# A conformer layer's gated tiles turned by VectorE through DRAM instead of by TensorE, with three smaller moves

## The chip, the core and the metric

One core of one Trainium2 chip runs the whole program. The metric is device time in microseconds (us), from runs of the whole program; the profile is one execution in which every instruction of every engine was recorded. The engines named below are PE (TensorE), DVE (VectorE), ACT (ScalarE), POOL (GpSimd) and SP (SyncE, which here only issues DMAs). Each engine works through its own instructions in order. DMAs issued by SP run in the hardware queue q1, those issued by ACT in q10.

## The reference, cut to what matters

Two layers on 256 latent and 256 context tokens (together the 512 rows below) with 1024 channels. Layer 0 mixes tokens with a conformer convolution, layer 1 with a bidirectional chunkwise mLSTM; each is followed by a squared-ReLU MLP.

```python
def conformer_conv(u, rows, w_pw1, b_pw1, w_dw, b_dw, ln_g, ln_b, w_pw2, b_pw2):
    a = u @ w_pw1 + b_pw1
    a = a[..., :CONV_DIM] * jax.nn.sigmoid(a[..., CONV_DIM:])
    a = dwconv(a, w_dw)                   # the latent part in rows of 64
    a = jax.nn.silu(layer_norm(a + b_dw, ln_g, ln_b))
    return a @ w_pw2 + b_pw2

def mlstm_chunk_scan(q, k, v, i_pre, f_pre, state):
    lf = jax.nn.log_sigmoid(f_pre)
    ...
        bcum = jnp.cumsum(lfc, axis=-1)
        dlog = bcum[..., :, None] - bcum[..., None, :] + ic[..., None, :]
    ...
```

## The kernel before, in words

**Products.** All weights are float32. A big weight arrives as `raw`, a piece of 1 MB (128 partitions x 2048). ACT casts each half of it to `wh` (L151), DVE forms the rest `wl` from `raw` and `wh` (L152), and PE does three matmuls for each product (L182, L185, L186, and L213 to L215 in the output-gate product of layer 1). `raw` has a few buffers, so SP can issue the load of a piece only when an older one was read for the last time.

**What sets the order.** The kernel is written as a program in one order; a tile scheduler then sets every engine's own order, and puts in the waits. `tc.issue_after(x)` holds an instruction behind x. Within an engine nothing overtakes: if SP's next DMA waits for PE, the DMAs behind it wait too.

**Start.** `vecs` holds all bias and norm vectors, 408 values on each partition. Its first 64 (L117) are the first DMA of the program, and the other 344 (172 KB; L657) are issued after the second start step. Behind that come eight start steps (`start0` to `start2`): for each 128 channels SP loads a piece of `ada_w`, of `xT` and of `pw1a`; PE makes the modulation (L344, tile `fl`), DVE and ACT build `u`, and PE adds to the first four groups of the pointwise product `pw1`.

**Pointwise product and gate.** The product gives 16 tiles of 128 channels x 512 tokens: for each f in 0 to 7 a gate (even group) and a value (odd group). `pw1_epi` passes the gate through a sigmoid (L791, ACT) and then multiplies the value with it (L795, DVE): that makes the gated tile `a`, channels on the partitions. The convolution works on the other layout, tokens on the partitions: tile `A` (128 x 4 x 1024). `turn(f, a)` does it: four PE transposes of 128x128 into PSUM (L806, tile `ln`), one ACT copy into `A` (L807). For f = 0 to 2 the call is put into the list `turns` and taken out when the next group ends. f = 0 to 3 are the first half of the channels (h = 0), f = 4 to 7 the second (h = 1).

**Convolution.** After f = 3 (and after f = 7) the half goes through forward transforms along the tokens: matmuls of `A` with tables (L830, `ge`, `lt`, `tab`, then L835), a product with the transformed taps on DVE (L849), and back (L860). `taps` builds the transformed filter by matmuls with a table (L741) and two ACT operations (L742). The modulation parts that come later in layer 0 (`ada_g1`, `ada_s2`) are matmuls L344 on `raw` pieces of `ada_w`, put between these steps; four more pieces of `ada_w` go into parts of `A` that are free again (L943).

**Layer 1.** The values of attention are already turned by DVE in 32x32 blocks into the tile `res` (L1261), stored in DRAM (`v_dr`, four DMAs by ACT for each set, L1265) and loaded again by SP. In the attention stage a generator `decay` makes log-decays from the gates on ACT and DVE (L1413 to L1428), their cumulative sums on PE (L1435, L1436), copies these back (L1437), scans (L1448), stores a row in DRAM (`ng_dr`) and loads it spread over the partitions (L1510, tile `L`). Each `yield` in `decay` gives the turn to the output-gate product (weights `wo`), which runs beside it, a half group of it per step. The residual `R`, 1 MB in the tile `res`, is loaded from `r_dr` at the start of the second of four parts, (h, d) = (0, 1) (L1573).

Of the kernel before, what the change touches and what calls it, by code (L numbers as in the profile page):

```python
# [8 lines left out]
F32 = mybir.dt.float32  # L9
# [62 lines left out]
def hybrid_kernel(ctx: ExitStack, tc: tile.TileContext, xT, vecs_d, wdw_d, ada0_w, ada_w, wg_d, pw1a, pw1, pw2, w1_0, w2_0,  # L72
# [12 lines left out]
    def nm(s):  # L85
        uid[0] += 1
        return f"{s}_{uid[0]}"
# [13 lines left out]
    def psum(tag="mm"):  # L101
        return pp.tile([P, 512], F32, tag=tag, name=nm(tag), bufs={"mm": 3, "ln": 2, "fl": 1, "cv": 2}[tag])
# [10 lines left out]


    vecs = con.tile([P, NV], F32, name="vecs")
    NV0 = _OFF["ada_b1"][0]
    nc.sync.dma_start(vecs[:, :NV0], vecs_d[:, :NV0])  # L117

    def V(name, i=0, n=1):
        o = _OFF[name][0]  # L120
# [533 lines left out]
    start1(0)  # L654
    idle(spare, 5)
    start0(1)
    nc.sync.dma_start(vecs[:, NV0:], vecs_d[:, NV0:])  # L657
    for f in range(DT):
        start2(f, (0,))
        if f + 1 < DT:  # L660
# [118 lines left out]
                              qtr.rearrange("p (b j c) -> p j b c", b=4, j=4)[:, :, :, 0:16])  # L779


    A = padp.tile([P, 4, D], F32, name="A")
    Y = [[U() for _ in range(2)] for _ in range(4)]
    bst = con.tile([P, 4, 2, 6], F32, name="bst")
    hold, mark = {}, {}

    def pw1_epi(m, ps):
        f, gate = m // 2, m % 2 == 0
        if gate:
            sg = tmp("E")  # L790
            mark["gate"] = nc.scalar.activation(sg, ps, AF.Sigmoid, bias=V("b_pw1", DT + f)).ins  # L791
            hold[f] = sg
            return
        a = hold.pop(f)
        nc.vector.scalar_tensor_tensor(a, ps, V("b_pw1", f), a, op0=ALU.add, op1=ALU.mult)  # L795
        if f < 3:
            turns.append(lambda: turn(f, a))
        else:
            turn(f, a)

    turns = []

    def turn(f, a):
        tr = psum("ln")
        for b in range(4):
            mark["tr"] = nc.tensor.transpose(tr[:, b * P:(b + 1) * P], a[:, b * P:(b + 1) * P], ident).ins  # L806
        nc.scalar.copy(A[:, :, f * P:(f + 1) * P], tr.rearrange("p (b c) -> p b c", b=4))  # L807
        if f == 3:
            with tc.issue_after(mark["tr"]):
                ada_g1.mm(first, range(4, 8))  # L810
            for tt in range(2):
                whole(tt, [psum() for _ in range(2)])
# [96 lines left out]
    ada_g1, ada_s2 = Ada(0, 4, 2), Ada(0, 6, 6)  # L909

    def pw1_next(m, ps):
        while turns:
            turns.pop(0)()
        if m == 3:
            first.extend(ada_load(0, 4))
            ada_g1.mm(first, range(4))
        if m == 11:
            ada_s2.mm(half + ada_load(0, 6 + ada_s2.n, halves=(1,)))
            with tc.issue_after(mark["gate"]):
                nc.scalar.activation(warm, eps, AF.Sqrt)  # L920
        if m in (5, 6):
            with tc.issue_after(lastmm[0]):
                back(0, m - 3, psum("cv"))
        pw1_epi(m + KO0, ps)
        if m in (1, 2):
            taps(m - 1)
        if m in (4, 6):
            unit = ada_g1 if m == 4 else ada_s2
            blocks = ada_load(0, unit.u0 + unit.n)
            with tc.issue_after(lastmm[0]):  # L930
                unit.mm(blocks)
        if m in (4, 5):
            whole(m - 2, [psum(), psum("ln")], True)
        if m == 5:
            ada_g1.end()
        if m == 8:
            for i, tag in enumerate("SLSL"):
                half.append(tmp(tag))
                nc.sync.dma_start(half[i], ada_w[0, 6 + ada_s2.n, 0, :, i * 512:(i + 1) * 512])
        if m == 10:  # L940
            pw2_raw.extend(raw_load(pw2[g, 0]) for g in range(2))
            for i in range(4):
                nc.sync.dma_start(A[:, i, 0:512], ada_w[0, 10, 0, :, i * 512:(i + 1) * 512])  # L943
# [244 lines left out]
    for _ in side:  # L1188
        pass

    def rows_tile():
        return xp.tile([P, 2, D], F32, tag="res", name=nm("res"), bufs=1)

    r_dr = dp.tile([P, 2, D], F32, name="r_dr")
    R = rows_tile()
    for f in range(0, DT, 2):
# [195 lines left out]
    def decay(_):  # L1392
        gT = tmp("L")
        nc.scalar.copy(gT, gps)
        yield
        gk = psum("ln")
        for b in range(4):
            nc.tensor.matmul(gk[:, b * 16:(b + 1) * 16], gT[:, b * P:(b + 1) * P], foldg, start=True, stop=True)
        gs = tmp("S")[:, 0:64].rearrange("p (b c) -> p b c", b=4)
        nc.vector.tensor_tensor(gs, gk[:, 0:64].rearrange("p (b c) -> p b c", b=4),  # L1400
                                VA("b_gate").rearrange("p (b c) -> p b c", b=4), op=ALU.add)
        gb_ = [tmp("L"), tmp("E"), tmp("E")]
        g8 = [gb_[i // 3][:, (i % 3) * 4 * NG:(i % 3 + 1) * 4 * NG].rearrange("p (b c) -> p b c", b=4) for i in range(8)]
        ig, fg, bsb, ex, up1, cor, lf, fa = g8
        nc.vector.memset(ig, 0.0)
        nc.vector.memset(fg, 0.0)
        for d in range(2):
            nc.vector.tensor_copy(ig[:, :, 32 * d:32 * d + 4], gs[:, :, 8 * d:8 * d + 4])
            nc.vector.tensor_copy(fg[:, :, 32 * d:32 * d + 4], gs[:, :, 8 * d + 4:8 * d + 8])


        nc.vector.scalar_tensor_tensor(fa, fg, -1.0, fg, op0=ALU.mult, op1=ALU.max)
        nc.scalar.activation(ex, fa, AF.Exp, scale=-1.0)  # L1413
        nc.vector.tensor_scalar(up1, ex, 1.0, None, op0=ALU.add)
        nc.vector.scalar_tensor_tensor(cor, up1, -1.0, ex, op0=ALU.add, op1=ALU.subtract)
        nc.scalar.activation(lf, up1, AF.Ln)
        nc.vector.reciprocal(up1, up1)
        nc.vector.tensor_tensor(cor, cor, up1, op=ALU.mult)
        nc.vector.tensor_tensor(lf, cor, lf, op=ALU.subtract)
        nc.vector.tensor_scalar(fa, fg, 0.0, None, op0=ALU.min)  # L1420
        nc.vector.tensor_tensor(lf, lf, fa, op=ALU.add)

        nc.vector.memset(up1, 0.0)
        for d, (b0, b1, b2, b3) in ((0, (0, 1, 2, 3)), (1, (1, 0, 3, 2))):
            c = slice(32 * d, 32 if d == 0 else NG)
            nc.vector.tensor_copy(up1[:, b1, c], lf[:, b0, c])
            nc.vector.tensor_tensor(up1[:, b2, c], up1[:, b1, c], lf[:, b1, c], op=ALU.add)
            nc.vector.tensor_tensor(up1[:, b3, c], up1[:, b2, c], lf[:, b2, c], op=ALU.add)  # L1428
        yield
        yield  # L1430
        bps = psum("ln")
        for d, cum in ((0, upper), (1, lower)):
            c = slice(32 * d, 32 if d == 0 else NG)
            reg = bps[:, 0:4 * NG].rearrange("p (b c) -> p b c", b=4)[:, :, c]
            nc.tensor.matmul(reg, cum, lf[:, :, c], start=True, stop=False)  # L1435
            nc.tensor.matmul(reg, ones, up1[:, :, c], start=False, stop=True)  # L1436
        nc.vector.tensor_copy(bsb, bps[:, 0:4 * NG].rearrange("p (b c) -> p b c", b=4))  # L1437
        nc.vector.tensor_tensor(acol, ig, bsb, op=ALU.subtract)

        yield  # L1440
        aT = psum("ln")
        for b in range(4):
            nc.tensor.transpose(aT[:NG, b * P:(b + 1) * P], acol[:, b, :], ident)
        aR, mR = tmp("S"), tmp("S")
        nc.vector.tensor_copy(aR[:32, :], aT[:32, :])
        nc.vector.tensor_copy(aR[32:NG, LO], aT[32:NG, LO])
        nc.vector.tensor_copy(aR[32:NG, HI], aT[32:NG, T - 1:C - 1:-1])
        nc.vector.tensor_tensor_scan(mR[:NG, :], aR[:NG, :], aR[:NG, :], 0.0, op0=ALU.max, op1=ALU.max)  # L1448
        nc.vector.tensor_scalar(negm[:32, :], mR[:32, HI], -1.0, None, op0=ALU.mult)
        nc.vector.tensor_scalar(negm[32:NG, :], mR[32:NG, T - 1:C - 1:-1], -1.0, None, op0=ALU.mult)  # L1450
        nc.scalar.dma_start(ng_dr, negm)
        bsbs.append(bsb)
        yield
# [112 lines left out]
    def gate_o(h):  # L1566

        for d in range(2):
            bo = rows(BO().rearrange("p a b -> p (a b)"), bo_d[h:h + 1, d * DH:(d + 1) * DH])
            pss = [psum() for _ in range(2)]  # L1570
            if (h, d) == (0, 1):
                with tc.issue_after(loaded[0]):
                    nc.sync.dma_start(R, r_dr)  # L1573
            for q in range(4):
# [383 lines left out]
def _cols(v):  # L1958
    return v.reshape(-1, P).T
# [6 lines left out]
def _layout(np, i):  # L1966
    g = {k: np.asarray(v) for k, v in i.items()}
    a, turned = {}, _turned(np)
    a["xT"] = np.concatenate([g["ctx"][0], g["x"][0]], axis=0).T
    vec = {  # L1970
        "c_ctx": _cols(g["c_ctx"]), "c": _cols(g["c"][0]),
        "b_pw1": _cols(g["conv_b_pw1"][0]),
        "cln_g": _cols(g["conv_ln_g"][0]), "cln_b": _cols(g["conv_ln_b"][0]),
        "b_pw2": _cols(g["conv_b_pw2"][0]), "b_conv": _cols(g["ml_b_conv"][0]),
        "w_conv": g["ml_w_conv"][0].T.reshape(ET, P, QTAP).transpose(1, 0, 2).reshape(P, ET * QTAP),
# [12 lines left out]
    wg = g["ml_w_gate"][0].reshape(3, H, DH, 16)  # L1988
    wg = np.stack([wg[0], wg[1], wg[2][:, turned]])
    a["wg_d"] = wg.reshape(3, ET, P, 16).transpose(0, 2, 1, 3).reshape(3, P, 256)  # L1990
    pw1 = g["conv_w_pw1"][0].reshape(D, 2, DT, P).transpose(0, 2, 1, 3)[:, :, ::-1, :].reshape(D, 2 * D)
    a["pw1a"] = pw1[:, :512].reshape(DT, P, 512)
    a["pw1"] = _blocks(pw1[:, 512:])
    a["pw2"] = _blocks(g["conv_w_pw2"][0])
# [39 lines left out]
```

## Time and profile before

| | |
|---|---|
| three runs, us | 1663.55, 1664.04 (median), 1665.42 |
| the profiled execution | 1665.14 us, of which the recorded span is 1663.4 us |
| busy in the span, us | PE 1648.7, DVE 1038.1, ACT 734.6, POOL 14.4 |
| granted TensorE clock | full in all forty slices of the page |
| DMA | 303.70 MB, mean 183 GB/s |

The time around the span is 1.7 us, and the profiled execution is 1.1 us above the median. In the views, a row of the timeline begins with the start in us from the span's start and the duration; `[1.63 <-DVE E L1421]` says that the engine was idle for 1.63 us before and what released it. A PE matmul on float32 operands stands in the trace as two records: `fl x4` of the program is `x8` in the timeline.

### The profile page before, as it was taken

What the parts mean: (1) busy time and instruction counts of PE and PEld (TensorE: products, weight loads), DVE (VectorE), ACT (ScalarE), POOL (GpSimd) and SP (SyncE); (2) the same over time, 40 slices, a digit from 0 to 9 for tenths busy, and PEclk for the clock granted to TensorE, in tenths of its full rate; (3) what the DMA queues carried; (4) which work ended last, traced back from release to release, by engine and by line L of the source; (5) the groups of instructions that cost most, each with busy time, mean ns of one, the idle gap of its engine ahead of it and who ended that gap; (6) DMA issues with size and microseconds to landing.
All of it is one profiled execution on the core that took longest, in us unless ns stands there. A gap on an engine that the chain in (4) does not pass through costs nothing.

```text
span 1663.4 us, 22731 instructions
## 1 busy us (share of the span) xinstructions
PE 1648.7 (99%) x8856; PEld 1357.6 (82%) x8856; DVE 1038.1 (62%) x1863; ACT 734.6 (44%) x1182; POOL 14.4 (1%) x64
## 2 busy tenths in 40 slices
PE   9999999999999999999999999999999999999998
PEld 6665898888888998877787899888877888878886
DVE  6554895666535765762354753553489876776677
ACT  4313573232324476652233533442477654555453
POOL 0000000000000000000000000000000000000001
PEclk9999999999999999999999999999999999999999
DMA  9555223534324065557774852554465555675552
GB/s 353 208 210 214 92 75 111 167 123 148 136 101 152 4 228 194 184 196 266 278 259 146 302 179 79 179 194 144 148 240 197 203 215 203 250 284 183 178 194 85
DMA packets 74331, 303.70 MB, mean 183 GB/s; under 512 B 7694, under 2 KB 23858, under 8 KB 44144
## 3 DMA queue, kind: packets, MB, share of 16 engines
q1 hardware_dynamic: 56368, 286.49, 49.1%
q10 hardware_dynamic: 17856, 15.77, 2.8%
q8 instruction: 69, 1.13, 0.3%
q14 instruction: 38, 0.31, 0.1%
HBM read 285.42 MB, written 16.81 MB: 182 GB/s over the span
## 4 chain that ended last, share of the span: by engine, by line
PE 95%; DVE 2%; DMA 1%; ACT 1%; issue 0%; SPq 0%; DVEq 0%; ACTq 0%
PE mm L182 18%; PE mm L185 17%; PE mm L186 17%; PE mm L197 7%; PE mm L198 4%; PE mm L215 3%; PE mm L213 3%; PE mm L214 3%; PE cv L213 2%; PE cv L215 2%; PE cv L214 2%; PE fl L344 1%; PE ln L182 1%; PE cv L860 1%; PE ln L214 1%; PE ln L185 1%
## 5 line engine op out<-in xcount | busy, mean ns | idle before, releaser
L152 DVE TENSOR_TENSOR wl<-raw,wh 128x1024 fp32r<-128x1024 f32 x344 | 418.7, 1221 | 245.5 <-ACT wh L151 233.4
L151 ACT CAST wh<-raw 128x1024 fp32r<-128x1024 f32 x344 | 358.6, 1051 | 469.3 <-PE mm L185 244.4
L185 PE MATMUL mm<-u,wh 128*128 128x512 f32 (+1 forms) x808 | 291.5, 361 | 0.2 <-DVE u L604 0.2
L182 PE MATMUL mm<-u,wh 128*128 128x512 f32 (+1 forms) x680 | 243.8, 359 | 0.0
L186 PE MATMUL mm<-u,wl 128*128 128x512 f32 (+1 forms) x680 | 241.3, 355 | 0.0
L185 PEld LDWEIGHTS mm<-u,wh 128*128 128x128 f32 x808 | 152.7, 189 | 23.2 <-issue 1.0
L182 PEld LDWEIGHTS mm<-u,wh 128*128 128x128 f32 x680 | 128.4, 189 | 24.4 <-issue 6.3
L186 PEld LDWEIGHTS mm<-u,wl 128*128 128x128 f32 x680 | 128.5, 189 | 17.8
L213 PE MATMUL mm<-wh,xl 128*128 128x512 f32 x256 | 101.0, 395 | 0.7 <-DVE og L1588 0.7
L182 PE MATMUL mm<-xm,wh 128*128 128x512 f32 x256 | 101.0, 394 | 0.0
L215 PE MATMUL mm<-wl,xl 128*128 128x512 f32 x256 | 100.0, 393 | 0.0
L214 PE MATMUL mm<-wh,xl 128*128 128x512 f32 x256 | 99.9, 390 | 0.0
L186 PE MATMUL mm<-xm,wl 128*128 128x512 f32 x256 | 99.7, 389 | 0.0
L182 PE MATMUL mm<-hid,wh 128*128 128x512 f32 (+1 forms) x256 | 93.3, 364 | 0.0
L186 PE MATMUL mm<-hid,wl 128*128 128x512 f32 (+1 forms) x256 | 92.8, 363 | 0.0
L185 PE MATMUL mm<-hid,wh 128*128 128x512 f32 (+1 forms) x256 | 92.8, 363 | 0.0
L197 PE MATMUL mm<-x,wh 128*128 128x512 f32 x232 | 81.1, 398 | 0.0
L185 PE MATMUL mm<-qq,wh 128*128 128x272 f32 x256 | 73.9, 289 | 0.0
L182 PE MATMUL mm<-qq,wh 128*128 128x272 f32 x256 | 73.5, 288 | 0.0
L186 PE MATMUL mm<-qq,wl 128*128 128x272 f32 x256 | 73.5, 288 | 0.0
L197 PE MATMUL mm<-u,wh 128*128 128x512 f32 x192 | 68.6, 399 | 0.0
L1099 DVE SCALAR_TENSOR_TENSOR x<-mm,ada,x 128x256 f32<-128x256 f32 x64 | 28.5, 479 | 63.4 <-PE mm L186 63.4
(537 smaller groups left out, 3249.4 us busy)
## 6 DMA issues: line engine op xcount, KB each, us to landing
raw<-w SPq DMA_DIRECT2D x64, 1024.0 KB, 4.9
raw<-wo SPq DMA_DIRECT2D x32, 1024.0 KB, 4.9
raw<-ada_w SPq DMA_DIRECT2D x22, 1024.0 KB, 7.0
ar<-ada_w SPq DMA_DIRECT2D x80, 256.0 KB, 3.9
raw<-wv SPq DMA_DIRECT2D x16, 1024.0 KB, 8.0
raw<-wqT SPq DMA_DIRECT2D x16, 1024.0 KB, 5.7
raw<-wq SPq DMA_DIRECT2D x16, 1024.0 KB, 5.8
raw<-wk SPq DMA_DIRECT2D x16, 1024.0 KB, 5.2
```

The costliest lines, as they stand in the source:

```text
L151: c = nc.scalar.copy(hi, src)
L152: lastsub[0] = nc.vector.tensor_tensor(lo, src, hi.bitcast(F32), op=ALU.subtract).ins
L182: a = nc.tensor.matmul(ps, wh, xh, start=start, stop=False)
L185: nc.tensor.matmul(ps, wh, xl, start=False, stop=False)
L186: lastmm[0] = nc.tensor.matmul(ps, wl, xh, start=False, stop=stop).ins
L197: todo = [lambda s_, e_: nc.tensor.matmul(ps, wh, r[0], start=s_, stop=e_), lambda s_, e_: nc.tensor.matmul(ps[:, :n], wl, r[0][:, :n], st ...
L198: lambda s_, e_: nc.tensor.matmul(ps[:, :n], wl, r[0][:, :n], start=s_, stop=e_)]
L213: nc.tensor.matmul(ps, xh, wh, start=start, stop=False)
L214: nc.tensor.matmul(ps, xl, wh, start=False, stop=False)
L215: nc.tensor.matmul(ps, xh, wl, start=False, stop=stop)
L344: a = mark_unit[0] = nc.tensor.matmul(ps[32 * j:32 * j + 32], cs[:, kt, 14 - 2 * v:46 - 2 * v], blocks[kt], start=first and kt < 4, stop=l ...
L1099: nc.vector.scalar_tensor_tensor(res[m][:, sl_], p_, g[:, m:m + 1], res[m][:, sl_], op0=ALU.mult, op1=ALU.add)
```

## The change

Four parts.

1. `vecs` is loaded whole, 128 x 408, as the first DMA; the later load of 344 columns is gone.
2. The gated tiles f = 0, 1, 2 and 4, 5, 6 aren't turned by PE. DVE transposes each in blocks of 32x32 into the tile `res` (`vturn3`). After the third of a half, ACT issues four stores into DRAM (`a_dr`; runs of 96 values, 384 bytes), which set the rows right, and one DMA loads 128 x 4 x 384 into `A`: for the first half issued by SP, for the second by ACT, behind the sigmoid of f = 7. The columns of `w_pw1` and `b_pw1` are permuted on the host within the 384 channels of a half so that they come out in order. f = 3 and 7 go by PE as before. The list `turns` is gone.
3. `decay` has one more `yield` ahead of its cumulative sums.
4. The load of `R` goes from (h, d) = (0, 1) to (1, 1).

```diff
     vecs = con.tile([P, NV], F32, name="vecs")
-    NV0 = _OFF["ada_b1"][0]
-    nc.sync.dma_start(vecs[:, :NV0], vecs_d[:, :NV0])
+    nc.sync.dma_start(vecs, vecs_d)
...
     start0(1)
-    nc.sync.dma_start(vecs[:, NV0:], vecs_d[:, NV0:])
...
+    def rows_tile():
+        return xp.tile([P, 2, D], F32, tag="res", name=nm("res"), bufs=1)
+
     A = padp.tile([P, 4, D], F32, name="A")
+    a_dr = [dp.tile([P, 4, 3 * P], F32, name=f"a_dr{h}") for h in range(2)]
...
         nc.vector.scalar_tensor_tensor(a, ps, V("b_pw1", f), a, op0=ALU.add, op1=ALU.mult)
-        if f < 3:
-            turns.append(lambda: turn(f, a))
+        if f % 4 == 3:
+            turn(f, a)
         else:
-            turn(f, a)
-
-    turns = []
+            vturn3(f, a)
+
+    three = []
+
+    def vturn3(f, a):
+        h, m = divmod(f, 4)
+        if m == 0:
+            three.append(rows_tile().rearrange("p a b -> p (a b)")[:, 0:12 * P].rearrange("p (t q m j) -> p t q m j", q=4, m=3, j=32))
+        vk = three[-1]
+        nc.vector.transpose(vk[:, :, :, m, :], a)
+        if m == 2:
+            for r in range(4):
+                nc.scalar.dma_start(a_dr[h][:, :, r * 96:r * 96 + 96].rearrange("(q j) t x -> j t q x", j=32),
+                                    vk[32 * r:32 * r + 32].rearrange("j t q m i -> j t q (m i)"))
+            if h == 0:
+                with tc.issue_after(loaded[0]):
+                    nc.sync.dma_start(A[:, :, 0:3 * P], a_dr[0])
...
     def pw1_next(m, ps):
-        while turns:
-            turns.pop(0)()
...
+        if m == 10:
+            with tc.issue_after(mark["gate"]):
+                nc.scalar.dma_start(A[:, :, 512:512 + 3 * P], a_dr[1])
...
         yield
         yield
+        yield
         bps = psum("ln")
...
-            if (h, d) == (0, 1):
+            if (h, d) == (1, 1):
                 with tc.issue_after(loaded[0]):
                     nc.sync.dma_start(R, r_dr)
...
+    glu = np.arange(D)
+    for h in (0, 512):
+        glu[h:h + 384] = h + np.arange(384).reshape(4, 3, 32).transpose(1, 0, 2).reshape(384)
...
-        "b_pw1": _cols(g["conv_b_pw1"][0]),
+        "b_pw1": _cols(g["conv_b_pw1"][0].reshape(2, D)[:, glu].reshape(-1)),
...
-    pw1 = g["conv_w_pw1"][0].reshape(D, 2, DT, P).transpose(0, 2, 1, 3)[:, :, ::-1, :].reshape(D, 2 * D)
+    pw1 = g["conv_w_pw1"][0].reshape(D, 2, D)[:, :, glu].reshape(D, 2, DT, P).transpose(0, 2, 1, 3)[:, :, ::-1, :].reshape(D, 2 * D)
```

Lines of the changed kernel differ in number from those of before: L741 becomes L739, L806 L822, L830 L846, L860 L876, L1419 L1433, L1421 L1435, L1435 L1450.

How the schedule moves, at three places. First, SP's own order ahead of the first forward transform. `raw_852` and `raw_854` are two pieces of `ada_w`, `raw_940` is a piece of `pw1`. Before:

```order
L939 DMA L_1063<-ada_w 128x512
L145 DMA raw_852<-ada_w 128x2048
L939 DMA L_1067<-ada_w 128x512
L145 DMA raw_854<-ada_w 128x2048
L145 DMA raw_940<-pw 128x2048
L943 DMA A<-ada_w 128x512 x2
```

Now (the same pieces are called `raw_844`, `raw_846` and `raw_928`):

```order
L956 DMA L_1046<-ada_w 128x512
L144 DMA raw_844<-ada_w 128x2048
L817 DMA A<-a_dr_586 128x4x384
L144 DMA raw_846<-ada_w 128x2048
L144 DMA raw_928<-pw 128x2048
L956 DMA L_1050<-ada_w 128x512
```

The new load of `A` stands directly behind `raw_844`, which takes over the buffer of `raw_750` and so can be issued only after PE has read that piece for the last time (`fl_754<-raw_750` in the next rows).

Second, PE's order at the same place, from the end of the pointwise group to the first forward transform. Before:

```order
L186 MATMUL mm_685<-u_473,wl_731 128x512
L344 MATMUL fl_762<-raw_758,cs 32x512 x4
L806 MATMUL ln_768<-ident,E_722 128x128 x4
L344 MATMUL fl_762<-raw_760,cs 32x512 x4
L830 MATMUL mm_779<-A,ge_560 128x512
```

Now:

```order
L185 MATMUL mm_683<-u_472,wl_723 128x512
L343 MATMUL fl_754<-raw_750,cs 32x512 x4
L739 MATMUL ln_716<-L_575,tab 128x512
L739 MATMUL ln_719<-L_575,tab 128x512
L822 MATMUL ln_760<-ident,E_714 128x128 x4
L343 MATMUL fl_754<-raw_752,cs 32x512 x4
L846 MATMUL mm_771<-A,ge_559 128x512
```

The second pair of tap matmuls, which stood at the head of this pointwise group, now stands between the two modulation steps; the first pair, in the group before, moved 14 matmuls later. Between the reading of `raw_750` and the first use of `A` lie two tap matmuls, the turn of f = 3 and one modulation step.

Third, DVE's order in `decay`, from the reciprocal to the log-decays, of which PE's cumulative sums are made. Before:

```order
L1417 RECIPROCAL E_10713<-E_10713 128x144
L152 TENSOR_TENSOR wl_10910<-raw_10877,wh_10909 128x1024
L1418 TENSOR_TENSOR E_10713<-E_10713 128x144
L1419 TENSOR_TENSOR E_10714<-E_10713,E_10714 128x144
L1423 MEMSET E_10713 128x144
L1421 TENSOR_TENSOR E_10714<-E_10714 128x144
```

Now:

```order
L1431 RECIPROCAL E_10696<-E_10696 128x144
L151 TENSOR_TENSOR wl_10885<-raw_10854,wh_10884 128x1024
L1432 TENSOR_TENSOR E_10696<-E_10696 128x144
L151 TENSOR_TENSOR wl_10928<-raw_10925,wh_10927 128x1024
L1433 TENSOR_TENSOR E_10697<-E_10696,E_10697 128x144
L1437 MEMSET E_10696 128x144
L1435 TENSOR_TENSOR E_10697<-E_10697 128x144
```

One more `wl`, of the next weight piece, stands ahead of the log-decays. PE's first cumulative sum (L1435, now L1450) stands five matmuls later among those of the output gate.

More of the change, by code (lines that the diff above doesn't have):

```diff
@@ L1189, in hybrid_kernel @@
         pass
-    def rows_tile():
-        return xp.tile([P, 2, D], F32, tag="res", name=nm("res"), bufs=1)
     r_dr = dp.tile([P, 2, D], F32, name="r_dr")
```

## The prediction

> **What bounds the kernel now.** I began with the page's busy times and the waits of PE.
>
> ```profile
> PE 1648.7 (99%) x8856; PEld 1357.6 (82%) x8856; DVE 1038.1 (62%) x1863; ACT 734.6 (44%) x1182; POOL 14.4 (1%) x64
> ```
>
> ```profile
> PE ln L1435 <- DVE E L1421: 1.6, 1, 1.6
> PE fl L344 <- DMA raw<-ada_w: 1.4, 2, 1.2
> PE cv L176 <- DVE ones L130: 1.1, 1, 1.1
> PE mm L213 <- DVE og L1588: 0.7, 1, 0.7
> PE ln L741 <- issue: 0.6, 1, 0.6
> ```
>
> PE works 1648.7 of 1663.4 us, and all its waits longer than half a microsecond are in these five rows. So PE is the bound everywhere: an instruction taken from PE counts in full, work moved to DVE, ACT or the queues counts only where it makes PE wait, and what can be won from waits is small. The rest is therefore read as a list: what PE loses, and the places at which it must now wait.
>
> **Part 1, PE's turns.** The chain of waits runs through PE at the turns. Its pieces, with start and length:
>
> ```profile
> 50.68 0.87 PE ln L806 x8
> ...
> 65.22 0.44 PE ln L806 x4
> 65.65 1.94 PE ln L741 x4
> ...
> 101.39 0.59 PE ln L806 x4
> ...
> 120.12 0.44 PE ln L806 x4
> ...
> 131.48 0.44 PE ln L806 x4
> ```
>
> The x8 is f = 0 and 1, then f = 2, 4, 5 and 6. What goes is 0.87 + 0.44 + 0.59 + 0.44 + 0.44 = **2.78 us**. ACT's copies go too, but ACT, at 44%, doesn't set the end here.
>
> **Part 2, the start.** 172 KB of `vecs` leave this place in SP's queue and go ahead of the first weight piece:
>
> ```profile
> 4.39 0.44 SPq L657 DMA_DIRECT2D vecs<-vecs_d  x1
> ```
>
> ```profile
> 0.00:20.00 20.00, 17.45 (x138) 13.71 (x142) 10.86 (x47) 9.98 (x19) 2.52 (x13) 1.00 0.90 355
> 76.00:78.00 2.00, 2.00 (x5) 0.90 (x6) 0.13 (x1) 0.00 (x0) 0.00 (x0) 1.00 0.95 393
> ```
>
> The last figure of a row is GB/s. PE's first two modulation steps wait for `ada_w` (1.4 us above), and the queues are 90% busy, so the two pieces land later by 176,000 bytes at 355 to 393 GB/s, 0.45 to 0.50 us. From the third step on the same bytes are ahead as before, but PE, which then works without waits, keeps its lateness. I take **+0.4**, a little less since the first microseconds are partly latency; 0.2 to 0.6.
>
> **Part 3, DVE's three blocks and the taps.** The nearest rows for the new operations are the same kind of transpose of the same shape in layer 1, and its stores:
>
> ```profile
> L1261 DVE STREAM_TRANSPOSE res<-vt x16: 702/706/714, 735.1 to 914.9; 128x512 f32<-128x512 f32 x16
> ```
>
> ```profile
> 57.29 0.42 DVE L715 SCALAR_TENSOR_TENSOR tab<-F,tab 128x256 f32<-128x256 f32 x1
> 57.64 0.74 DVE L795 SCALAR_TENSOR_TENSOR E<-mm,vecs,E 128x512 f32<-128x512 f32 x1
> ```
>
> L715 finishes the table of the taps, for which PE already waits 0.6 us (L741). In DVE's new order three transposes and the product of f = 2 stand ahead of it: 3 x 0.71 + 0.74 = 2.9 us, so the table is ready at 57.71 + 2.9 = 60.6 at the latest. PE comes to the taps 14 matmuls of 0.23 us later, less the removed 0.87: 57.24 + 3.2 - 0.87 = 59.6. The wait grows from 0.6 to at most 1.0; **+0.3**, 0 to 0.6.
>
> **Part 4, the first half of `A`.** This is the largest term. PE and SP before:
>
> ```profile
> 73.21 1.06 PE L344 MATMUL fl<-raw,cs 128*32 128x512 f32 x8
> ...
> 75.84 1.13 PE L830 MATMUL mm<-A,ge 128*128 128x512 f32 x2
> ```
>
> ```profile
> 74.33 0.33 SPq L145 DMA_DIRECT2D raw<-ada_w  x1
> ```
>
> SP's load is issued at 74.33, just as PE is through with the first modulation step (73.21 + 1.06). In the new order this step starts earlier, by the turns (0.87 + 0.44) and by the second pair of taps (1.94), which now follows it, and later by the two terms above (0.7): it ends at 74.27 - 3.25 + 0.7 = 71.7. Only then can `raw_844` be issued, and the load of `A` is directly behind it. How long do they take?
>
> ```profile
> raw<-wo SPq DMA_DIRECT2D x32, 1024.0 KB, 4.9
> ...
> A<-ada_w SPq DMA_DIRECT2D x4, 256.0 KB, 3.0
> ```
>
> A piece of 1 MB alone lands in 4.9 us, at 76.6; 768 KB (0.79 million bytes) more in the same queue at 393 GB/s take 2.0 us more: `A` lands at 78.6. PE arrives at its first forward transform at 75.84 - 1.31 + 0.7 = 75.2. It waits **3.4 us**. If the two loads shared the queues evenly, twice the 768 KB would have to pass in front: some 77.9, a wait of 2.7; runs of 1536 bytes that go a third slower than the big ones would make it 4.4. The stores don't decide here: ACT casts the weight piece that landed at 61.35 first, then issues them:
>
> ```profile
> 61.35 1.05 ACT L151 CAST wh<-raw 128x1024 fp32r<-128x1024 f32 x1 [8.98 <-DMA raw<-pw]
> ```
>
> ```profile
> 915.69 2.78 ACTq L1265 DMA_DIRECT2D v_dr<-res  x4
> ```
>
> ```profile
> DMA to landing us min/median/max: 3.6/6.3/10.3
> ```
>
> (the last for `v_dr`, the stores of layer 1). The fourth store begins at 62.4 + 2.1 = 64.5 and lands at 70.8, ahead of 71.7. The weights of the next group are no part of it: their casts begin at 61.35, and PE begins that group behind the transforms. So this wait eats all that parts 1's first three turns gave.
>
> **Part 5, the second half.** Here ACT issues the load, and no big piece is ahead of it, but the stores decide:
>
> ```profile
> 130.45 0.75 DVE L795 SCALAR_TENSOR_TENSOR E<-mm,vecs,E 128x512 f32<-128x512 f32 x1 [3.42 <-PE mm L186]
> ```
>
> ```profile
> 145.05 1.13 PE L830 MATMUL mm<-A,ge 128*128 128x512 f32 x2
> ```
>
> The tile f = 6 is ready at 131.2, turned at 131.9; the fourth store begins 2.1 us later and lands after 6.3: 140.3 to 141. A load of 768 KB lies between 3.0 us (256 KB) and 4.9 (1 MB): 4.3. It lands at 144.6 to 145.3. PE, from that same tile on, loses only one turn and arrives at 145.05 - 0.44 = 144.6. A wait of 0 to 1.8, **+0.8**; ACT is held meanwhile, but only the copy of f = 7 and casts with much slack are behind it.
>
> **Part 6, decay and `R`.** The rows, PE, DVE, SP and ACT:
>
> ```profile
> 1216.40 0.49 PE L1435 MATMUL ln<-E,tri 128*128 128x128 f32 x2 [1.63 <-DVE E L1421]
> ```
>
> ```profile
> 1214.25 1.19 DVE L152 TENSOR_TENSOR wl<-raw,wh 128x1024 fp32r<-128x1024 f32 x1
> ...
> 1231.93 0.48 DVE L1525 SCALAR_TENSOR_TENSOR S<-L,acol,mask 128x256 f32<-128x256 f32 x1 [2.53 <-DMA L<-ng_dr]
> ```
>
> ```profile
> 1214.41 1.05 ACT L151 CAST wh<-raw 128x1024 fp32r<-128x1024 f32 x1 [0.22 <-DMA raw<-wo]
> ```
>
> ```profile
> 1232.00:1290.00 58.00, 57.32 (x261) 46.20 (x260) 54.74 (x117) 45.41 (x78) 0.00 (x0) 1.00 0.58 202
> ```
>
> The later sums are meant to meet the log-decays ready. But one more `wl` of 1.19 us now stands ahead of these on DVE, and five matmuls (1.15 us) more ahead of PE's sums: the wait of 1.6 stays. What changes is that two `wl` more are done before L1525; they fit into its idle time of 2.53, and the row in DRAM is written only some 0.4 later. DVE then enters the stretch in which it is 94% busy (54.74 of 58) almost 2 us ahead, and PE's wait of 0.7 for `og` can go. The cast for that extra `wl` waits for the piece of `wo` that came behind `R` (1214.41); with `R` gone from there it lands 2.7 us (1 MB at 393 GB/s) earlier, in time. I take **-0.3**: at best both waits go with part of the first (-1.6), at worst the extra `wl` comes a cast later (+1.2).
>
> **The sum.** -2.78 + 0.4 + 0.3 + 3.4 + 0.8 - 0.3 = **+1.8 us**. The profiled execution took 1665.14, so it would be 1666.9; that execution is 1.1 above the median of the runs, and for the median I forecast 1664.04 + 1.8 = **1665.8 us**.
>
> [...]
>
> **The rivals.**
>
> *Faster: the loads of `A` come in time.* If SP's load of `A` were in effect not held by `raw_844` (part 4 without its wait), as the even sharing that makes the wait shrink allows in part, then -2.78 + 0.4 + 0.3 + 0 - 1.3 = -3.4: 1660.6. For it: the stores have landed by 70.8, before PE arrives. Against it: the order of SP and the wait of `raw_844` for PE, which the row at 74.33 shows at work.
>
> *Slower: the stores of 384 bytes are slow.* If each lands after 10.3 us, the longest of `v_dr`, in place of 6.3, the second half lands at 131.9 + 2.1 + 10.3 + 4.3 = 148.6 and PE waits 4.0; in the first half the last store lands at 74.8, `A` at 79.1, a wait of 3.9. In all +1.8 + 3.2 + 0.5 = +5.5: 1669.5. It decides from a landing of 6.9 us on in the second half, which has almost no room. [...] Against it: the stores have 192 KB each, those of `v_dr` 256.
>
> *Slower by `R`.* Its 1 MB now goes between the `wo` pieces near 1264, where DVE and ACT are busy and the pieces have little lead; it can hold one up by the 2.7 us that it takes: +1.8 + 2.5, 1668.3. Against it: DMA is at 58% in that stretch.
>
> **How the numbers follow.** The forecast has 0.50, the loads in time 0.20, slow stores 0.22, `R` 0.08. A difference of less than 0.2% (3.3 us) can't be told from none here. The forecast's own ends are -2.78 + 0.2 + 0 + 2.7 + 0 - 1.6 = -1.5 and -2.78 + 0.6 + 0.6 + 4.4 + 1.8 + 1.2 = +5.8, most of it within 3.3: 0.42 the same, 0.08 slower. The first rival is faster (0.20), the second slower (0.22), the third half and half. So faster 0.20, same 0.46, slower 0.34. The range takes the lower rival nearly and the upper whole: 1661.0 to 1669.8.
>
> **What would show it.** Right: among PE's waits a new one of about 3.4 us, the first L846 for the load of `A`; one below 2 at the second; no L822 but the two of f = 3 and 7; the first modulation step 0.4 later; L1450 still waiting about 1.6. Wrong: no wait at the first L846 (the first rival), over 3 us at the second (the second), waits for `wl` after 1264 (the third). A wait that grows elsewhere, at a place where only the order changed, would break the sum from outside.

## The result and the profile after

The changed kernel takes 1667.71 us (median of 16 runs, 1665.46 to 1670.31), the kernel before beside it 1664.37 us (16 runs, 1662.74 to 1666.54): ratio 1.0020, 95% interval 1.0013 to 1.0027, so 3.3 us slower. The forecast was +1.8 and 1665.8. The profiled execution has a span of 1667.4 us, 4.0 more than that of before.

PE's waits after the change:

```profile
PE mm L846 <- DMA A<-a_dr: 6.4, 2, 3.8
PE cv L175 <- DVE ones L129: 1.1, 1, 1.1
PE mm L212 <- DVE og L1603: 0.4, 1, 0.4
PE ln L739 <- DVE tab L713: 0.3, 1, 0.3
```

The rows stand as in the prediction: total us, times, longest. The two waits for `A` are new, the one for the log-decays (L1435, now L1450) is gone, and the waits at the start, for `og` and for the taps are shorter. But the waits alone don't make up the loss. PE's timeline around the first of them:

```profile
72.37 1.07 PE L343 MATMUL fl<-raw,cs 128*32 128x512 f32 x8
77.20 1.46 PE L846 MATMUL mm<-A,ge 128*128 128x512 f32 x2 [3.77 <-DMA A<-a_dr]
78.46 1.91 PE L846 MATMUL mm<-A,lt 128*128 128x512 f32 x2
80.17 1.55 PE L846 MATMUL mm<-A,tab 96*128 96x512 f32 x2
81.55 1.88 PE L846 MATMUL mm<-A,ge 128*128 128x512 f32 x4
83.36 1.08 PE L876 MATMUL cv<-F,tab 128*64 128x512 f32 x4
```

After 3.77 us of waiting the first ten transform matmuls (ten records of the trace, five matmuls of the program) take 83.36 - 77.20 = 6.16 us; before they took 4.50 (75.84 to the first L860 at 80.34). The stretches say why; the column behind the five engines is the granted TensorE clock, then the DMA share and GB/s:

```profile
77.00:78.00 1.00, 0.80 (x2) 0.53 (x3) 0.00 (x0) 0.00 (x0) 0.00 (x0) 0.90 1.01 426
78.00:79.00 1.00, 1.00 (x2) 0.33 (x1) 0.00 (x0) 0.00 (x0) 0.00 (x0) 0.50 1.01 426
79.00:80.00 1.00, 1.00 (x2) 0.33 (x1) 0.00 (x0) 0.00 (x0) 0.00 (x0) 0.50 1.03 434
80.00:81.00 1.00, 1.00 (x2) 0.33 (x1) 0.59 (x1) 0.00 (x0) 0.00 (x0) 0.50 1.00 426
81.00:82.00 1.00, 1.00 (x4) 0.50 (x3) 0.95 (x3) 0.00 (x0) 0.00 (x0) 0.89 0.74 287
```

PE ran at half its clock for 0.2 + 3 + 0.2 = 3.4 us and lost half of that, 1.7 us. The second wait was followed by the same: from 149.27 to 156.29, 7.02 us, for what took 5.35 before (145.05 to 150.40).

```profile
149.27 1.84 PE L846 MATMUL mm<-A,ge 128*128 128x512 f32 x2 [2.64 <-DMA A<-a_dr]
```

```profile
149.00:150.00 1.00, 0.73 (x1) 0.30 (x2) 0.59 (x1) 0.00 (x0) 0.00 (x0) 0.74 0.91 328
150.00:151.00 1.00, 1.00 (x3) 0.43 (x2) 0.00 (x0) 0.00 (x0) 0.00 (x0) 0.50 1.03 412
151.00:152.00 1.00, 1.00 (x3) 0.48 (x2) 0.00 (x0) 0.00 (x0) 0.00 (x0) 0.50 0.92 379
152.00:153.00 1.00, 1.00 (x2) 0.43 (x2) 0.14 (x1) 0.00 (x0) 0.00 (x0) 0.55 1.08 426
```

PE's place in the two traces, at the same instructions:

| | before | after | late by |
|---|---|---|---|
| third modulation step of the start | 15.06 | 14.63 | -0.4 |
| first forward transform begins | 75.84 | 77.20 | 1.4 |
| first back transform | 80.34 | 83.36 | 3.0 |
| forward transform of the second half | 145.05 | 149.27 | 4.2 |
| back transform of the second half | 150.40 | 156.29 | 5.9 |
| end of the span | 1663.4 | 1667.4 | 4.0 |

From 156 us to the attention stage nothing changes; there and behind it 1.9 us come back, 1.7 of them between 1210 and 1300 us.

### The profile page after: what moved, and what is told of

It reads as the page before. It is cut to its first block, busy times and chain, and to the rows that moved or that the text cites. A ratio compares the mean times of both kernels' runs of the same rounds, so it can differ in the third digit from the quotient of the medians.

```text
span 1667.4 us, 22696 instructions
## 1 busy us (share of the span) xinstructions
PE 1649.5 (99%) x8832; PEld 1357.8 (81%) x8832; DVE 1039.9 (62%) x1869; ACT 731.7 (44%) x1176; POOL 14.3 (1%) x64
## 4 chain that ended last, share of the span: by engine, by line
PE 93%; DVE 3%; DMA 2%; issue 0%; ACT 0%; SPq 0%; ACTq 0%; DVEq 0%
PE mm L181 17%; PE mm L184 17%; PE mm L185 17%; PE mm L196 7%; PE mm L212 4%; PE mm L214 4%; PE mm L197 4%; PE mm L213 4%; PE cv L212 2%; PE cv L214 2%; PE cv L213 2%; PE fl L343 1%; PE ln L181 1%; PE cv L876 1%; PE ln L184 1%; PE fl L765 1%
```

## The experiments

Four theories were to be told apart: that SP's order makes the first wait; that PE's slow stretch is its clock (or, instead, the DMAs at over 400 GB/s beside it); which of parts 3 and 4 gives back the time in the attention stage; and whether one load of `vecs` costs anything. The runs came in three jobs on two chips; each job ran the kernel before as well (medians 1664.99, 1664.83 and 1663.78, in 33, 28 and 14 runs), and the ratios are to that.

**e1, PE kept at work in the waits.**

```diff
+                xfs = [psum() for _ in range(2)]
+                if tt == 0:
+                    with tc.issue_after(mark_unit[0].ins):
+                        idle(xfs[1], 16)          # the second half: 12
-                whole(tt, [psum() for _ in range(2)])
+                whole(tt, xfs)
```

> The changed kernel, with 16 and 12 matmuls of ones by ones put ahead of the first forward transform of each half, so that PE works while it waits for A; the transforms overwrite what they write. Theory (the clock): after the two waits of 3.8 and 2.6 us PE runs for 3.4 us at half its clock, 1.7 us lost each time. Then the first ten transform matmuls take 4.5 us in place of 6.2, the granted clock stays at 1.00 throughout, and the time falls by about 3.4 us, to 1664.3. Rival (contention): the matmuls are slow since the DMAs write into A and the weight buffers at over 400 GB/s at that moment. Then they stay at 6.2 us, and the time at 1667.7.

Measured: 1665.35 us (1664.67 to 1665.65), ratio 1.0002 (0.9993 to 1.0011); the changed kernel had 1.0020. PE in its trace, and one stretch:

```profile
73.42 3.84 PE L175 MATMUL mm<-ones 128*128 128x128 f32 x32
77.10 1.03 PE L850 MATMUL mm<-A,ge 128*128 128x512 f32 x2
77.97 1.02 PE L850 MATMUL mm<-A,lt 128*128 128x512 f32 x2
78.82 1.02 PE L850 MATMUL mm<-A,tab 96*128 96x512 f32 x2
79.69 1.88 PE L850 MATMUL mm<-A,ge 128*128 128x512 f32 x4
81.50 1.94 PE L880 MATMUL cv<-F,tab 128*64 128x512 f32 x8
```

```profile
78.00:79.00 1.00, 1.00 (x4) 0.52 (x3) 0.00 (x0) 0.00 (x0) 0.00 (x0) 1.00 0.96 401
```

The transforms begin when they began in the changed kernel (77.10 against 77.20), so useful work waits as long; but they take 4.40 us in place of 6.16, at full clock, while the DMAs move nearly as much (401 GB/s in that microsecond, 426 in the changed kernel). That is the clock, and contention falls.

The time came down by some 3 us by the ratios (0.0018 of 1665), a little less than the 3.4 expected. The mean clock of the runs gives a likely reason. In the profiles of before and of the changed kernel PE is through 8.2 us before the end, and the clock falls to half for the last 3.8 and 5.8 us of the span (from 1659.59 and 1661.59; the digits of a page, where 9 is 90% or more, hide that). An estimate from these numbers: a run without any other such stretch has a mean of 0.998 or 0.999, one stretch of 3.4 us takes 0.001 more away, and a run at 0.997 or below had one at least. The ten runs of e1 have 0.998 or 0.999; the sixteen of the changed kernel have 0.996 in eight, 0.997 in five and 0.998 in three, so probably not every one of them had both stretches.

**e2, the load of `A` ahead of `raw_844`.**

```diff
-                    nc.sync.dma_start(A[:, :, 0:3 * P], a_dr[0])
+                    mark["aload"] = nc.sync.dma_start(A[:, :, 0:3 * P], a_dr[0]).ins
...
-            blocks = ada_load(0, unit.u0 + unit.n)
+            with tc.issue_after(mark["aload"]):
+                blocks = ada_load(0, unit.u0 + unit.n)
```

> The changed kernel, with SP's load of the first half of A ahead of raw_844 in place of behind it; nothing else moves. Theory (SP's order makes the first wait): the load is issued when the stores have landed, about 68 us, and lands at 73, when PE arrives; the first wait of 3.8 us falls under 0.5, its half clock goes too, and the time falls by about 5.3 us, to 1662.4. Rival (the stores make the wait): A still lands at 76 or later, the wait stays above 2.5 us and the time above 1666. Second rival (the wait moves): raw_844 lands 2 us later and the next modulation step waits for it; the time falls by under 2.5 us.

Measured: 1661.46 us (1660.22 to 1665.93; 1662.4 expected), ratio 0.9987 (0.9977 to 0.9996). SP, and PE at the first transform:

```profile
66.02 0.62 SPq L817 DMA_DIRECT2D A<-a_dr  x1
70.08 1.30 SPq L144 DMA_DIRECT2D raw<-ada_w  x2
```

```profile
72.45 1.07 PE L343 MATMUL fl<-raw,cs 128*32 128x512 f32 x8
73.45 1.13 PE L846 MATMUL mm<-A,ge 128*128 128x512 f32 x2
```

```profile
PE mm L846 <- DMA A<-a_dr: 1.2, 1, 1.2
```

Issued at 66.0 in place of 70.5, the load is hidden: PE goes from the modulation step to the transform without a pause, and what is left is the second wait, 1.2 us. So the stores had landed by 66.0, and the place of one DMA in SP's order made the first wait. Three of the ten runs took 1662.5 to 1665.9 at a mean clock of 0.996 to 0.997, the others up to 1661.6 at 0.998 or 0.999. So, by the estimate above, the clock still falls in some of its runs. Whether that is behind the second wait isn't shown: in its own profile, at a mean of 0.998, what follows that wait up to the back transform takes 5.32 us (142.40 to 147.72; 5.35 before), and the taps are another place for such a stretch (last section).

**e3, everything but the turns.** Before, with the three edits of parts 1, 3 and 4.

> The kernel before with parts 1, 3 and 4 of the change (vecs in one load, decay's sums a half step later, R later), PE turning all eight tiles. By the two traces: start -0.5 us, decay -1.6, the stretch behind it -0.4: 2.3 to 2.5 us faster than before, ratio 0.9985. By the sums on record (+0.4 for the start, -0.3 for decay): no difference, 1664.5.

Measured: 1663.63 us (1662.44 to 1667.92), ratio 0.9998 (0.9989 to 1.0007): no difference that the runs could tell, and the 0.9985 of the theory lies outside the interval. The one trace looks like the theory all the same: its span is 1660.9, PE is 0.3 us ahead of before up to the attention stage and 2.0 us ahead after it, and the wait for the log-decays is gone. But a trace is one execution, and e4 shows that this gain also comes without parts 3 and 4.

**e4, the turns alone.** The changed kernel with parts 1, 3 and 4 taken back.

> The kernel before with part 2 alone, the six tiles by DVE. By the two traces (PE is 5.9 us late at 200 us, 6.4 if the start gains nothing): 6 to 6.5 us slower, 1670.5, with both waits for A and two stretches at half clock. By the sum on record (-2.78 + 0.3 + 3.4 + 0.8): +1.7, 1666.

Measured: 1667.11 us (1664.26 to 1670.24), ratio 1.0016 (1.0006 to 1.0025), between the two expectations. The 1670.5 that the two traces gave lies outside the interval. In its profile PE waits 4.4 and 1.3 us for `A`; the clock falls to half at 62.12, behind the taps, and at 79.18, behind the first wait, but not behind the second (the mean is 0.997). In the attention stage it is the kernel before, `R` and the sums in their old places and order. All the same the wait of 1.6 us for the log-decays is gone (PE's first sum has none), and ACT waits 1.25 us for the piece of `wo` ahead of it, where in before it waited 3.21:

```profile
1219.87 0.49 PE L1451 MATMUL ln<-E,tri 128*128 128x128 f32 x2
```

```profile
1210.14 2.00 ACT L151 CAST wh<-raw 128x1024 fp32r<-128x1024 f32 x2 [1.25 <-DMA raw<-wo]
```

PE, 5.1 us late up to 1215 us, is 3.5 late at 1220 and 3.6 at the end. So the 1.9 us that come back in the changed kernel's trace are no proof for parts 3 and 4.

**e5, the sums a half step later, alone; e6, R later, alone.**

```diff
e5:      yield
+        yield
         bps = psum("ln")
e6: -            if (h, d) == (0, 1):
    +            if (h, d) == (1, 1):
```

> The kernel before with part 3 alone, the one more yield. In its schedule neither PE's first cumulative sum nor DVE's log-decays stand elsewhere than before, so by the theory that part 4 makes the gain: PE's wait of 1.6 us for the log-decays stays, and the time is that of before, within 0.3 us of 1664.5. Rival (part 3 makes the gain): the wait is gone, 1.6 to 2 us faster.

> The kernel before with part 4 alone, R loaded at (1, 1). In its schedule the extra wl and the five matmuls come with it, as in the changed kernel. Theory (part 4 makes the gain, since the pieces of wo land 1.5 us earlier when R is not among them): PE's wait for the log-decays goes from 1.6 us to under 0.2, the casts after the wait for wo start at 1205.5 in place of 1207.0, and the time falls by 1.8 to 2.2 us. Rival (part 3 is needed): the wait stays above 1 us, and the time falls by under 0.7.

Measured: e5 1664.16 us, ratio 0.9997 (0.9988 to 1.0006); e6 1664.26, ratio 0.9999 (0.9990 to 1.0008). By the times neither can be told from before; the traces tell them apart. PE's first sum, in e5 and then in e6:

```profile
1217.22 0.49 PE L1436 MATMUL ln<-E,tri 128*128 128x128 f32 x2 [0.99 <-DVE E L1421]
```

```profile
1217.05 0.49 PE L1435 MATMUL ln<-E,tri 128*128 128x128 f32 x2
```

And the cast of the second piece of `wo` on ACT, in e5 and in e6:

```profile
1207.85 2.00 ACT L151 CAST wh<-raw 128x1024 fp32r<-128x1024 f32 x2 [2.58 <-DMA raw<-wo]
```

```profile
1206.62 2.00 ACT L151 CAST wh<-raw 128x1024 fp32r<-128x1024 f32 x2 [1.65 <-DMA raw<-wo]
```

With `R` gone the piece lands earlier (e6 is 0.3 us ahead of e5 at this point, so by 0.9 of the 1.2), the two moves that the order showed, one more `wl` and five matmuls, come with part 4 and not with part 3, and PE doesn't wait: against before it is 1.15 us late at 1200 us and 0.5 ahead at 1300, 1.65 us won. In e5, whose order is that of before, a wait of 1.0 remains. But that wait isn't the same in each execution: with `R` at its old place and the same order of instructions there it was 1.6 in before, 1.0 in e5, 0.5 in e8, and under 0.2 in e4 and e9. In the six profiles with `R` at its new place it was under 0.2 each time. So the new place may make the wait rarer, but the 1.65 us measure one long wait of before's profile, and the 1.8 to 2.2 us expected of e6 lie outside the interval of its times.

**e7, two tiles in the second half.** e2, with f = 4 and 5 by DVE and f = 6 and 7 by PE:

```diff
+    NT = (3, 2)
-        if f % 4 == 3:
+        if f % 4 >= NT[f // 4]:
...
-        if m == 2:
+        if m == NT[h] - 1:
...
-                nc.scalar.dma_start(A[:, :, 512:512 + 3 * P], a_dr[1])
+                nc.scalar.dma_start(A[:, :, 512:512 + 2 * P], a_dr[1])
```

> Run e2 (SP's load of the first half ahead of raw_844), and in the second half only f = 4 and 5 by DVE, f = 6 and 7 by PE; rows of 64 values (256 bytes) in the stores, the columns permuted to suit. The tile f = 5 is ready 11 us ahead of f = 6. Theory: the load of the second half lands before PE arrives, the wait of 1.2 us of e2 goes, one turn of 0.44 comes back: 0.7 us faster than e2, some 4 us faster than before, and no half clock at either half in any run. Rival (stores of 256 bytes are slow): landing above 9 us from issue and the second wait above 1 us.

Measured: 1659.78 us (1659.46 to 1660.27), ratio 0.9968 (0.9957 to 0.9980): 5.05 us faster than before and the best of all; its median is 1.7 below that of e2, which ran in another job on the other chip. Its second half, and the landings of its stores and loads of `a_dr`:

```profile
140.71 1.07 PE L343 MATMUL fl<-raw,cs 128*32 128x512 f32 x8
141.71 1.12 PE L848 MATMUL mm<-A,ge 128*128 128x512 f32 x2
```

```profile
DMA to landing us min/median/max: 2.9/3.8/8.4
```

No wait for `A` at either half, and by the estimate in e1 no slow stretch: the profile's mean clock is 0.999. Its six runs lie within 0.8 us, the 28 of before in the same job within 4.2.

**e8, vecs in one load, alone.**

> The kernel before with part 1 alone, vecs in one load. By the profiles so far (first modulation step at 6.59, 6.33, 6.59 and 6.62 us with one load, 6.89 and 6.58 with two; third step at 14.57 to 14.78 against 15.06 and 14.78): no more than 0.3 us either way, the first step at 6.3 to 6.7 us. By the sum on record: 0.4 us later, the first step at 7.3.

Measured: 1664.04 us, ratio 1.0000 (0.9991 to 1.0010). The first modulation step begins at 6.53 us, and PE is 0.2 to 0.5 us ahead of before from there to the attention stage, not 0.4 behind. One load shows no cost; the times alone couldn't have told 0.4 us.

**e9, the taps' wait filled.** Before, with three matmuls of ones ahead of the first tap matmuls.

> The kernel before with three matmuls of ones ahead of the first pair of tap matmuls, which overwrite what they write; PE waits there for 0.6 us and then works for 2 us on matmuls of 31 rows. In two of the profiles of kernels with PE's turns (e5, e6) and in e4 the granted clock fell to 0.5 for 3.4 us right behind this place, in those of before, e3 and e8 it did not; the runs of before spread over 5 us. [...]

Measured: 1665.36 us (1664.64 to 1667.46), ratio 1.0011 (1.0002 to 1.0020). Inconclusive. The author expected that, if the wait brings the half clock at the taps, filling it spares the stretch and takes time off. The mean clock was 0.999 in ten of its eleven runs and 0.998 in one, where before had 0.997 in four of fourteen, which fits; but the time rose. The scheduler also put other instructions elsewhere (PE waits 0.5 us each at two new places late in the program), so the times can't be compared for the taps alone.

## Why the prediction came out as it did

The direction and the range held: +3.3 us, where +1.8 was forecast, 1661.0 to 1669.8. That the sum came out near is in part luck: parts 4 and 5 were some 5.6 us dearer in the trace than forecast, parts 2, 3 and 6 some 3.0 cheaper. Of the signs that the prediction named for being right, the first wait (3.8 us) and the turns left to PE (f = 3 and 7) came; the second wait was 2.6 and not below 2, the first modulation step came 0.3 earlier (6.59 against 6.89) and not 0.4 later, and the wait of 1.6 at L1450 was gone.

| step | forecast | the runs |
|---|---|---|
| part 1, turns | -2.78 | went as said; in e2, without the first wait, PE is 3.9 ahead of before at 145 us, the start and the taps counted in |
| part 2, start | +0.4 | -0.4 in the trace, nothing in e8 |
| part 3, taps | +0.3 | the wait fell from 0.6 to 0.3: -0.3 |
| part 4, first half | +3.4 | 3.8 of wait and 1.7 of half clock |
| part 5, second half | +0.8 | 2.6 of wait and 1.7 of half clock (1.2 and 1.3 of wait and no half clock behind it in the profiles of e2 and e4) |
| part 6, decay and R | -0.3 | -1.9 in the trace; nothing that the runs could tell in e3 and e6 |

**Part 4** named the mechanism, the place and nearly the size: `raw_844` issued when PE is through with `raw_750`, `A` directly behind it.

```profile
70.00 0.33 SPq L144 DMA_DIRECT2D raw<-ada_w  x1
70.51 0.62 SPq L817 DMA_DIRECT2D A<-a_dr  x1
```

`A` landed 6.56 us after its issue (77.07, forecast 78.6), and PE was there at 73.4 (forecast 75.2; both earlier since start and taps came out earlier). The step that failed is the price of a wait: the sum took it at its length. The profile of before gave no sign of more: its clock is at half nowhere ahead of 1659.59, not even behind its longest wait of 1.63 us. In the changed kernel the waits of 3.77 and 2.64 us were each followed by 3.42 us at half clock (from 77.80 and from 149.48), which cost 1.7 us each.

**Part 5** sized its load too small. Its +0.8 doesn't follow from its own rows either: landing at 144.6 to 145.3 and PE at 144.6 make a wait of 0 to 0.7. The stores did what was said: the tile was turned at 133.9, the last of four stores landed 8.8 us later (8.4 to 9.1 forecast).

```profile
133.95 2.67 ACTq L813 DMA_DIRECT2D a_dr<-res  x4
...
142.82 0.59 ACTq L941 DMA_DIRECT2D A<-a_dr  x1
```

But the load took 6.3 us, not the 4.3 read between 256 KB and 1 MB. In e1, e2 and e4 the same load took 5.0, 5.0 and 4.9: so about 0.7 us is a wrong size, and the rest is this execution's. Two queues share the stretch, here from 142 to 150 us:

```profile
q1 hardware_dynamic: 314, 0.79, 34.9%
q10 hardware_dynamic: 553, 0.80, 29.7%
...
raw<-ada_w SPq DMA_DIRECT2D x3, 1024.0 KB, 9.2
A<-a_dr ACTq DMA_DIRECT2D x1, 768.0 KB, 6.3
S<-ada_w SPq DMA_DIRECT2D x2, 256.0 KB, 5.6
L<-ada_w SPq DMA_DIRECT2D x2, 256.0 KB, 6.5
```

Packets, MB and share by queue, then the issues: four small pieces of `ada_w`, with big ones among them, were issued to q1 beside the one load in q10. The prediction said that no big piece is ahead of it, which was right, and took that for an empty road. But in e1 and e2 the first of the same pieces was issued 1.4 and 1.6 us behind the load (here 1.4), and it took 5.0; so they don't explain the 6.3 by themselves, and its cause stays open.

**Part 2** had the sign wrong: it moved bytes ahead of the first piece and let that piece land later by the same bytes. In every profile with one load the first step began at 6.3 to 6.6 us; with two loads it began between 6.4 and 7.0. The start varies more from run to run than the 172 KB would cost.

**Part 3** let the table be ready at 60.6 at the latest and PE arrive at 59.6; the table was ready at 59.2 and PE there at 59.0, so less of DVE's added work stood in the way than the bound had it.

**Part 6** followed the schedule rightly (five matmuls, one `wl`), and took the wait of 1.6 us in the one profile of before for a property of the kernel that would stay. Its length is one execution's: the wait is gone in e4 and e9 as well, whose kernels have neither part 3 nor part 4 and the order of before at this place. Part 3, the edit meant for this wait, changed nothing in the order (e5). What part 4 is worth in a typical run stays open; by the times of e6 it is under 1.7 us (ratio 0.9990 at the least).

**The rivals.** The loads in time (-3.4): not what happened, but e2 shows what it is worth: ratio 0.9987, 2 us under before even with the second wait. (That rival's sum has -1.3 in place of the +0.8 and -0.3 of parts 5 and 6 without a reason; with the forecast's own terms it would have been -1.6.) Slow stores: the median landing of the 384-byte stores, 192 KB each, was 2.9 us in the first half and 6.9 in the second, that of the 256-byte stores of e7, 128 KB each, 5.8, and that of `v_dr`'s 6.3. The same 384 bytes came at both ends, so it isn't the size of the runs that makes the difference between the halves; whether short runs have a price of their own isn't shown. `R` in its new place held nothing up: PE has no wait for `wl` of over 0.2 us after 1264.

## What to carry to other kernels

Where PE is the bound, a wait like the two here (3.8 and 2.6 us) should be priced at its length and up to 1.7 us more, and if it can't be removed it can be filled with matmuls that nothing reads (e1). A single wait in a single profile, like the 1.6 us for the log-decays, should be looked up in a second profile before a gain is built on it. A load that replaces work on the bound engine has to be placed in its queue by what the DMA ahead of it waits for: one position in SP's order was worth over 5 us here. Of several like pieces of work, move off the bound engine those whose results are wanted late, and leave the last one (f = 6 in e7) where it was.

## What the runs showed of the hardware

The half clock doesn't need a wait of 2.6 us. In the profile of e5, PE waits 0.6 us for the taps' table and then works for 2 us on matmuls of 31 rows:

```profile
57.68 1.95 PE L741 MATMUL ln<-L,tab 31*128 31x512 f32 x4 [0.60 <-issue]
```

```profile
58.00:59.00 1.00, 1.00 (x3) 0.37 (x2) 0.24 (x1) 0.00 (x0) 0.00 (x0) 1.00 0.11 43
59.00:60.00 1.00, 1.00 (x3) 0.44 (x2) 0.00 (x0) 0.00 (x0) 0.00 (x0) 0.75 0.06 25
60.00:61.00 1.00, 1.00 (x3) 0.72 (x3) 0.00 (x0) 0.00 (x0) 0.00 (x0) 0.50 0.22 61
```

From 59.50 the clock is at half for 3.4 us; the matmuls then follow each other every 0.43 us in place of 0.23, and 1.6 us are lost. The same stands in e6 (from 59.60, behind a wait of 0.55), and a little later in e4 (from 62.12, behind a wait of 0.31). In the profile of before PE waits as long, and the clock stays full:

```profile
57.82 1.95 PE L741 MATMUL ln<-L,tab 31*128 31x512 f32 x4 [0.58 <-issue]
```

```profile
60.00:80.00 20.00, 19.98 (x85) 11.93 (x83) 5.33 (x7) 6.27 (x9) 0.00 (x0) 1.00 0.47 163
```

In e3 and e8 the wait is 0.6 too, the mean clock 0.999, and there is no such stretch. So it differs from execution to execution whether such a wait brings it. By the estimate in e1 some runs of the kernel before pay for one (18 of its 75 have a mean clock of 0.997 or below), and that can account for part of the spread of its runs (1662.6 to 1668.0), though only for part: in the first job its fourteen runs at a mean clock of 0.999 alone reach from 1662.65 to 1665.87. Whether the wait, the slim matmuls or both bring the stretch, e9 didn't settle.

Nor does the clock fall at a fixed time behind a wait. In the changed kernel it falls 0.60 us after the first wait has ended (77.20 to 77.80) and 0.21 us after the second (149.27 to 149.48); at the taps it falls 1.8 us after the wait's end in e5, 2.2 in e6 and 2.6 in e4. In all of these PE waited for 0.31 to 3.77 us ahead of the stretch, while behind waits of 0.58 (the taps in before), 1.19 (e2) and 1.63 us (the log-decays in before) the clock stayed full. So the length of a wait alone doesn't tell whether it is paid a second time. What else decides it, and how long PE must idle for it, no run here shows.
